# A Hymba layer on one core: weights of the first half fetched three ahead and split in turn, short convolution weight by weight, output splits in quarters

## The chip, the cores and the metric

The kernel runs on one core of a Trainium2 chip. The metric is the device time of one execution in microseconds (us), taken as the median of several runs. One launch computes everything; nothing is computed on the host.

## The reference

One layer of a backbone that mixes a short gated convolution with a bidirectional mLSTM, and then has a feed-forward part. There are 128 context tokens and 2048 latent tokens with 1024 features, in float32. Cut to its core:

```python
h = rmsnorm(x, norm1) * (1 + scale1) + shift1
z = h @ w_in                                    # sc_b, sc_c, sc_x, q, k, v, o, gates
y_sc = sc_b * conv3(sc_c * sc_x, conv_sc_w, conv_sc_b)
h_m = mlstm_bidir(q, k, v, gates, C0, n0, m0)   # 4 heads of 128, chunks of 128 tokens, both directions
h_m = rmsnorm_per_head(h_m) * mh_norm * sigmoid(o)
x = x + gate1 * (concat(y_sc, h_m) @ w_out)
h2 = rmsnorm(x, norm2) * (1 + scale2) + shift2
up = conv3(h2 @ w_up)
x = x + gate2 * ((silu(g) * a) @ w_down)        # a, g are the halves of up
```

The mLSTM goes through the chunks of 128 tokens with a matrix state: each chunk's output takes an attention-like product inside the chunk, weighted by exponentials of the gates, and a product with the state; each chunk's gated sum of k and v then updates the state. The results are both token groups after a final norm and the context's final states.

## The kernel before

**Tiling.** Features lie on the 128 partitions, tokens along the free dimension. The 2176 tokens are cut into blocks `BL` of 384 (the last has 256). Blocks 0, 1, 2 (`BA`) are called the first half, 3, 4, 5 (`BB`) the second. Every matrix product takes both operands as a high and a low part (fp32r) and makes three products of them. `load_w` fetches a weight tile of 1024 x 128 (512 KB) to `wst` (L103, two buffers), takes the high part on ScalarE (`wh`, L105) and the difference on GpSimd in two pieces of 512 columns (`wl`, L108). `gemm` (L191 to L199) makes 8 x 3 = 24 matmuls (L196, L197, L198) into one PSUM bank `acc`; "block product" below means such a group of 24.

**Order of the work.** Everything is written as generators that yield after each block product, so that other work can be put between. The second half goes first: v and gates, k heads, q heads, short convolution, o heads. Then the first half: v and gates (`vg`, evacuated by `rv`, L338); the gate rows (`gate_phase`), whose logarithm is taken by two activations (L589, L590, each with a table load) and which transposes `fc` and `ic` (L598), with k heads between its steps. Then come two passes by `weave`, a software pipeline over 34 units (17 chunks x 2 pairs of heads):

- `Sums`: transposes of k (`S`, L697), their copy `kT` on ScalarE, the weighted values `vw` on VectorE (L701), the product `y` (L708) and the update of the state `sb` (L721).
- `Mix`: `load` issues the loads of k, q, v, the state and `R` (L742, the gate rows of a chunk, 512 KB broadcast to all partitions). `first` makes `S` = q k (L753), adds the mask to `R` on GpSimd (L754), takes four exponentials on ScalarE (L758) and two products on VectorE (L761, L762). `second` makes the output products `y` (L773, L775), takes the denominators (L783 to L785), and empties `y` through ScalarE (L790) and VectorE (L791) into `hv`, then takes the norm (L793 to L797). `third` transposes `hv` (L803), multiplies it with the o gate (L805) and writes it to `yD` (L808).

In step i of `weave` unit i does `first`, i-3 `third`, i-1 `second` and i+1 `load`; then block products of the `fill` generator follow: 12 of q heads, 12 of o heads, 36 of the short convolution and 32 of the output projection of blocks 0 to 3. `Sums` takes one per step, `Mix` one per step and one more in every third. So in `Mix` the steps carry 2, 1, 1.

**Buffers.** PSUM has four banks `acc`, one tile `y` of two banks (a bank for each head), one bank `S` and one bank `st`. Split weights have four buffers.

**Output projection.** `out_proj` takes its blocks in pairs. For a pair it loads `yD` (`xt`, L404), splits all eight features of both blocks on ScalarE and VectorE (`hH` L406, `hL` L407), then for each of eight weights makes both blocks' products. It adds the residual (L433), writes `xD` (L435) and sums squares (L440, L441). The statistics of a pair (`inv_rms`, L122 to L126) follow; for the last pair (4, 5) they are put off into the FFN, to its fifth product (index 4).

**FFN.** The up projection runs by seven products of half size (L938 to L940); the token sums they need are written to `tD` and loaded as `slots` (L252, L257, L258). One product of a pair of blocks is 24 matmuls of 272 columns. The down projection is at L1030 to L1032.

Each engine runs its instructions in the order the scheduler wrote, and SP issues all transfers from one queue in order; an issue that waits for a buffer holds what is behind it.

Of the kernel before, what the change touches and what calls it, by code (L numbers as in the profile page):

```python
# [18 lines left out]
P = 128  # L19
# [11 lines left out]
WN = 1056  # L31
BL = [(i, min(384, T - i)) for i in range(0, T, 384)]
# [21 lines left out]
def hymba_kernel(ctx: ExitStack, tc: tile.TileContext, I, O):  # L54
# [46 lines left out]
    def load_w(src, n=1024):  # L101
        st = wp.tile([P, WN], F32, name="wst", bufs=2)
        Q.dma_start(st[:, :n], src)  # L103
        wh = wp.tile([P, WN], F32R, name="wh")
# [11 lines left out]
    def inv_rms(ss, n, r):  # L116
        """r [n tokens as columns of 128] = rsqrt(mean + eps) from the partial sums ss [P, n]."""
# [10 lines left out]
    def spread(r, n):  # L128
        """PSUM [P, n]: the columns of r along the free dimension, on every partition."""
# [60 lines left out]

    def gemm(w, h, n):  # L191
        (wh, wl), (hH, hL) = w, h
        acc = pa.tile([P, 512], F32, name="acc")
# [66 lines left out]
    def weights(j):  # L260
        """The split weights of the seven products."""
# [29 lines left out]
    def stages():  # L291
        """Products of all units, in order, each with its weights."""
        for hf in range(2):
            for j in range(FT):
                for i, w in enumerate(weights(j)):
                    yield hf, j, i, w

    # ---------------------------------------------------------------- mixer
    ph2 = ExitStack()
    with ExitStack() as ph1:  # L300
        wp = ph1.enter_context(tc.tile_pool(name="wp", bufs=4))
        xp = ph1.enter_context(tc.tile_pool(name="xp", bufs=2))
        pa = ph1.enter_context(tc.tile_pool(name="pa", bufs=4, space=PSUM))
# [5 lines left out]
        rq = ph0.enter_context(tc.tile_pool(name="rq", bufs=2))  # L309
# [13 lines left out]
        def vg(blocks, hs, ws):  # L323
            for b in blocks:
                hH, hL = hs[b]
                for j in range(2):
                    for c in chunks(b):
                        o = c * P - BL[b][0]
                        acc = pa.tile([P, 512], F32, name="acc")
# [21 lines left out]
        def heads(blocks, hs, w0, dst, func, scale, by_block=False):  # L351
            if by_block:
                ws = [load_w(I["w_in"][w0 + h]) for h in range(H)]
# [5 lines left out]
            for h in range(H):  # L359
                w = load_w(I["w_in"][w0 + h])  # L360
# [4 lines left out]
        def shortconv(blocks, hs):  # L365
            for m in range(4):
                wc, wx, wb = (load_w(I["w_in"][o + m]) for o in (4, 8, 0))
                for b in blocks:
                    t0, n = BL[b]
                    acc = gemm(wc, hs[b], n)  # L370
                    cr = rq.tile([P, 384], F32, name="cr")
                    S.activation(cr[:, :n], acc[:, :n], AF.Copy)
                    yield
                    acc = gemm(wx, hs[b], n)
                    V.tensor_tensor(cr[:, :n], acc[:, :n], cr[:, :n], op=ALU.mult)
                    yr = rq.tile([P, 384], F32, name="yr")
                    S.activation(yr[:, :n], cr[:, :n], AF.Identity, bias=scw[:, m, 3:4], scale=scw[:, m, 1:2])
                    for s0, s1, v in spans(t0, t0 + n):
                        w = GW if v else P
                        uu = cr[:, s0 - t0:s1 - t0].rearrange("p (r w) -> p r w", w=w)  # L380
                        yy = yr[:, s0 - t0:s1 - t0].rearrange("p (r w) -> p r w", w=w)
                        V.scalar_tensor_tensor(yy[:, :, 1:], uu[:, :, :w - 1], scw[:, m, 0:1],
                                               yy[:, :, 1:], op0=ALU.mult, op1=ALU.add)
                        V.scalar_tensor_tensor(yy[:, :, :w - 1], uu[:, :, 1:], scw[:, m, 2:3],
                                               yy[:, :, :w - 1], op0=ALU.mult, op1=ALU.add)
                    yield
                    acc = gemm(wb, hs[b], n)
# [751 lines left out]
```

## Time and profile before

| | us |
|---|---|
| median of 3 runs | 2620.94 (2619.29 to 2621.29) |
| profiled execution, span from first to last instruction | 2622.1 |
| TensorE busy | 2539.1 (97%) |
| VectorE busy | 1501.3 (57%) |
| ScalarE busy | 1066.1 (41%) |
| GpSimd busy | 706.4 (27%) |
| mean granted TensorE clock | 0.988 of full |

The profiled execution's own time is its span of 2622.1 us; the page gives no time around it. PE is TensorE, PEld its weight loads, DVE VectorE, ACT ScalarE, POOL GpSimd, SP the queue that issues transfers. In a row of waits stands who waited, for which engine and tile, the total, how often and the longest, in us. In a row of the timeline stand start, length, engine, line, operation, output and inputs, and in brackets the idle time before and what ended it. In a row of a window stand its bounds and length, then the busy time of each engine with its instructions, the granted clock, the share of the DMA engines and GB/s.

### The profile page before, as it was taken

The page shows a single profiled execution, that of the slowest core. Times are in us where ns is not written, and L with a number is a line of the kernel's source. Part 1 is how long each engine was busy: PE and PEld are TensorE (multiplying, and loading weights), DVE is VectorE, ACT ScalarE, POOL GpSimd, SP SyncE. Part 2 cuts the span into 40 slices and gives each one's busy share as a digit, 9 for nine tenths or more (in the row PEclk, how much of TensorE's full clock was granted, in tenths as well). Part 3 has the DMA queues.
Part 4 walks back from the last instruction along what each step waited for, and adds up shares of the span by engine and source line. Part 5 has one row for each costly group of instructions (what it writes and reads, how often), then busy time and mean ns, then how long its engine had stood idle before and what let it go on. Part 6 is the DMA issues. An engine that isn't in the chain of part 4 may idle for free. (4 is left out here: it accounts for less than half of the span.)

```text
span 2622.1 us, 46918 instructions
## 1 busy us (share of the span) xinstructions
PE 2539.1 (97%) x18511; PEld 2519.2 (96%) x18511; DVE 1501.3 (57%) x2560; ACT 1066.1 (41%) x2028; POOL 706.4 (27%) x534
## 2 busy tenths in 40 slices
PE   8999999999988988899999999999999999999998
PEld 7999999999988988899999999999999999999998
DVE  3993242333457666797686669666666635353533
ACT  4521142322345454464454446554544523232411
POOL 2542242211333344221121112111111222232232
PEclk9999999999999999999999999999999999999999
DMA  8773142555467887854252224222222635454442
GB/s 280 250 254 101 57 140 85 155 180 155 152 195 242 253 256 235 267 195 139 84 178 91 79 79 165 83 83 82 83 83 90 234 113 184 156 179 150 149 139 77
DMA packets 223582, 403.25 MB, mean 154 GB/s; under 512 B 20722, under 2 KB 144770, under 8 KB 221698
## 3 DMA queue, kind: packets, MB, share of 16 engines
q1 hardware_dynamic: 223362, 400.25, 46.5%
q8 instruction: 145, 2.38, 0.4%
q14 instruction: 75, 0.61, 0.1%
HBM read 305.13 MB, written 95.04 MB: 153 GB/s over the span
## 5 line engine op out<-in xcount | busy, mean ns | idle before, releaser
L196 PE MATMUL acc<-hH,wh 128*128 128x384 f32 (+1 forms) x1536 | 516.4, 336 | 0.0
L198 PE MATMUL acc<-hH,wl 128*128 128x384 f32 (+1 forms) x1536 | 505.0, 329 | 0.0
L197 PE MATMUL acc<-hL,wh 128*128 128x384 f32 (+1 forms) x1536 | 504.7, 329 | 0.0
L938 PE MATMUL pa<-tH,wh 128*128 128x272 f32 x1408 | 410.1, 291 | 5.6 <-DVE raw L950 5.2
L940 PE MATMUL pa<-tH,wl 128*128 128x272 f32 x1408 | 409.3, 291 | 0.4 <-DVE wl L276 0.4
L1030 PE MATMUL d<-uh,wh 128*128 128x272 f32 x1408 | 406.0, 288 | 3.1 <-ACT raw L948 3.1
L939 PE MATMUL pa<-tL,wh 128*128 128x272 f32 x1408 | 407.1, 289 | 0.0
L1032 PE MATMUL d<-uh,wl 128*128 128x272 f32 x1408 | 406.9, 289 | 0.0
L1031 PE MATMUL d<-ul,wh 128*128 128x272 f32 x1408 | 404.4, 287 | 0.0
L276 POOL TENSOR_TENSOR wl<-st,wh 128x512 fp32r<-128x512 f32 x132 | 182.3, 1381 | 730.5 <-ACT wh L275 697.5
L108 POOL TENSOR_TENSOR wl<-wst,wh 128x512 fp32r<-128x512 f32 (+1 forms) x160 | 234.3, 1486 | 434.0 <-ACT wh L105 421.5
L196 PEld LDWEIGHTS acc<-hH,wh 128*128 128x128 f32 x1536 | 291.1, 190 | 1.5 <-issue 0.4
L197 PEld LDWEIGHTS acc<-hL,wh 128*128 128x128 f32 x1536 | 291.1, 189 | 1.0
L198 PEld LDWEIGHTS acc<-hH,wl 128*128 128x128 f32 x1536 | 290.5, 189 | 0.2 <-issue 0.2
L938 PEld LDWEIGHTS pa<-tH,wh 128*128 128x128 f32 x1408 | 266.8, 190 | 6.4 <-issue 5.7
L1030 PEld LDWEIGHTS d<-uh,wh 128*128 128x128 f32 x1408 | 266.9, 190 | 3.4 <-ACT raw L948 3.3
L939 PEld LDWEIGHTS pa<-tL,wh 128*128 128x128 f32 x1408 | 267.3, 190 | 0.0
L940 PEld LDWEIGHTS pa<-tH,wl 128*128 128x128 f32 x1408 | 266.6, 189 | 0.6 <-DVE wl L276 0.6
L1032 PEld LDWEIGHTS d<-uh,wl 128*128 128x128 f32 x1408 | 266.1, 189 | 0.1
L1031 PEld LDWEIGHTS d<-ul,wh 128*128 128x128 f32 x1408 | 265.3, 188 | 0.0
L993 POOL TENSOR_TENSOR wl<-st,wh 128x704 fp32r<-128x704 f32 x64 | 150.5, 2352 | 367.2 <-ACT wh L991 358.2
L884 DVE SCALAR_TENSOR_TENSOR tt<-raw,fw,tt 128x127 f32<-128x127 f32 (+4 forms) x264 | 245.7, 959 | 1.5 <-ACT tt L890 0.8
(215 smaller groups left out, 5031.6 us busy)
## 6 DMA issues: line engine op xcount, KB each, us to landing
st<-in_w_up SPq DMA_DIRECT2D x88, 512.0 KB, 4.4
st<-in_w_down SPq DMA_DIRECT2D x64, 704.0 KB, 4.2
wst<-in_w_in SPq DMA_DIRECT2D x48, 512.0 KB, 4.1
us<-uD SPq DMA_DIRECT2D x88, 272.0 KB, 4.4
R<-nD SPq DMA_DIRECT2D x34, 512.0 KB, 5.5
wm<-in_w_modr SPq DMA_DIRECT2D x32, 512.0 KB, 4.7
F<-tD SPq DMA_DIRECT2D x12, 1088.0 KB, 8.8
uD<-tt SPq DMA_DIRECT2D x22, 576.0 KB, 2.8
```

The source lines that it names most:

```text
L108: G.tensor_sub(wl[:, a:a + n // 2], st[:, a:a + n // 2], wh[:, a:a + n // 2].bitcast(F32))
L196: PE.matmul(acc[:, :n], w_h, hH[:, k, :n], start=(k == 0), stop=False)
L197: PE.matmul(acc[:, :n], w_h, hL[:, k, :n], start=False, stop=False)
L198: PE.matmul(acc[:, :n], w_l, hH[:, k, :n], start=False, stop=(k == KT - 1))
L276: (G if on_pool else V).tensor_sub(wl, a, wh.bitcast(F32))
L884: V.scalar_tensor_tensor(o, i, w, o, op0=ALU.mult, op1=ALU.add)
L938: PE.matmul(acc, wh[:, w], rh, start=(kk == 0 and i in (0, 1, 5)), stop=False, skip_group_check=True)
L939: PE.matmul(acc, wh[:, w], rl, start=False, stop=False, skip_group_check=True)
L940: PE.matmul(acc, wl[:, w], rh, start=False, stop=(kk == 3), skip_group_check=True)
L1030: PE.matmul(acc[b][:, :NB], wh[:, c], uh[:, q], start=(j == 0), stop=False)
L1031: PE.matmul(acc[b][:, :NB], wh[:, c], ul[:, q], start=False, stop=False)
L1032: PE.matmul(acc[b][:, :NB], wl[:, c], uh[:, q], start=False, stop=(j == FT - 1))
```

## The change

Nine things change; the products computed stay the same.

1. **Weights of the first half.** A class `Stream` fetches the weights in the order of their use, as long as fewer than three are fetched or split, and splits the next one when one is taken. `in_turn` ties a split to the last ScalarE and the last GpSimd instruction written so far: it stays behind these in its engine's order. Split weights have five buffers instead of four.
2. **Short convolution** goes through the blocks with one weight, then with the next, instead of through three weights in each block (`cr`, `yr`: four buffers).
3. **Output projection.** The order is weights 0 and 1 on the first block, then on the second, then weight by weight. `split_y` splits a block in quarters (two features each). The quarters of the second block come beside the first two products, the rest of them at once before its first; those of the next pair's first block beside the last four products of this one. Rows of x are loaded two products ahead.
4. **PSUM.** Three pools of one bank for `acc`, taken in turn (a fourth bank during the start); `y` is one bank per head in a ring of three.
5. **`Sums` and `Mix`** work per head on `y`, and in `Mix` the state update `sf` stands behind the evacuation.
6. **`weave`** takes 1, 0, 1 fills in `Sums` (by step modulo three, from step -1) and 2, 1, 2 in `Mix`.
7. **Late statistics** of the last pair come after the FFN's second product (index 1), with their instructions placed behind its last matmul.
8. The FFN's loads and weight sums move with these, as the scheduler orders them.
9. The scratch for dynamic DMA is set to 1024; texts in the code are dropped.

```diff
-    def load_w(src, n=1024):
+    def in_turn(f, *engines):
+        traced = nc.cur_bb.bb.instructions
+        n, last = len(traced), {}
...
+        r = f()
+        for i in traced[n:]:
+            if i.engine in last:
+                tc.add_manual_dep(i, last[i.engine], mybir.DependencyInfo(
+                    mybir.DependencyClass.NoSync, mybir.DependencyReason.DATA), reason="in turn")
...
+    class Stream:
+        def fill(self):
+            while len(self.st) + len(self.ws) < 3:
+                src = next(self.srcs, None)
...
+                self.st.append(fetch(src))
+        def split(self):
+            if self.st:
+                st = self.st.pop(0)
+                self.ws.append(in_turn(lambda: split_w(st), ET.Activation, ET.Pool))
+        def __call__(self):
+            self.fill()
+            if not self.ws:
+                self.split()
+            w = self.ws.pop(0)
+            self.split()
+            self.fill()
+            return w
...
-        wp = ph1.enter_context(tc.tile_pool(name="wp", bufs=4))
+        wp = ph1.enter_context(tc.tile_pool(name="wp", bufs=5))
-        pa = ph1.enter_context(tc.tile_pool(name="pa", bufs=4, space=PSUM))
+        pa = [ph1.enter_context(tc.tile_pool(name=f"pa{i}", bufs=1, space=PSUM)) for i in range(3)]
...
+        def split_y(b):
+            yH, yL = ys[b] = h_pair()
+            for kh in range(2):
+                yt = xp.tile([P, 4, 384], F32, name="xt")
+                Q.dma_start(yt[:, :, :n], yD[4 * kh:4 * kh + 4, :, t0:t0 + n].rearrange("k p t -> p k t"))
+                for k in range(4):
+                    S.activation(yH[:, 4 * kh + k, :n], yt[:, k, :n], AF.Copy)
+                    V.tensor_sub(yL[:, 4 * kh + k, :n], yt[:, k, :n], yH[:, 4 * kh + k, :n].bitcast(F32))
+                    if k % 2:
+                        yield
...
+                order = [(0, b0), (1, b0), (0, b1), (1, b1)] + [(m, b) for m in range(2, KT) for b in (b0, b1)]
...
+                    if i < 2:
+                        run(islice(splits[b1], 2))
+                    elif after is not None and i >= 12:
+                        splits.setdefault(after, split_y(after))
+                        next(splits[after], None)
...
+        py = phr.enter_context(tc.tile_pool(name="py", bufs=3, space=PSUM))
...
-                pk = pm.tile([P, 2, 512], F32, name="y")
+                pk = [py.tile([P, 512], F32, name="y") for _ in range(2)]
...
-                y = pm.tile([P, 2, 512], F32, name="y")
+                ys = [py.tile([P, 512], F32, name="y") for _ in range(2)]
...
-                next(fill, None)
-                if extra and i % extra == 0:
+                for _ in range(blocks[i % 3]):
                     next(fill, None)
...
-        weave([Sums(c, hp) for c in range(NL - 1, -2, -1) for hp in range(2)], fill, 0)
-        weave([Mix(c, hp) for c in range(-1, NL) for hp in range(2)], fill, 3)
+        weave([Sums(c, hp) for c in range(NL - 1, -2, -1) for hp in range(2)], fill, (1, 0, 1))
+        weave([Mix(c, hp) for c in range(-1, NL) for hp in range(2)], fill, (2, 1, 2))
...
-            if late and i == 4:
-                late.pop()()
...
+            if late and i == 1:
+                with tc.issue_after(mm.ins):
+                    late.pop()()
```

At the start of the gates ScalarE had the splits `wh` of the first weights between the evacuations `rv` of the values, ahead of the two gate activations (`fe`, table load and activation twice). Before:

```order
L338 ACTIVATE rv<-acc 128x2x128 x12
L105 ACTIVATE wh<-wst 128x1024
L338 ACTIVATE rv<-acc 128x2x128
L105 ACTIVATE wh<-wst 128x1024
L338 ACTIVATE rv<-acc 128x2x128 x2
L105 ACTIVATE wh<-wst 128x1024
L338 ACTIVATE rv<-acc 128x2x128
L105 ACTIVATE wh<-wst 128x1024
L589 ACT_TABLE_LOAD
L589 ACTIVATE fe<-fe 128x136
L590 ACT_TABLE_LOAD
L590 ACTIVATE fe<-fe 128x136
```

Now, on the same engine at the same place (the lines are L393, L155, L672 and L673):

```order
L393 ACTIVATE rv<-acc 128x2x128 x16
L672 ACT_TABLE_LOAD
L672 ACTIVATE fe<-fe 128x136
L673 ACT_TABLE_LOAD
L673 ACTIVATE fe<-fe 128x136
L155 ACTIVATE wh<-wst 128x1024 x2
L403 ACTIVATE row<-acc 128x384 x3
```

The splits of the first weights went behind both gate activations. On TensorE, the transpose of `fc` stood behind two block products of the k head (the rows are the end of the second); `ic` followed three matmuls later:

```order
L198 MATMUL acc<-hH,wl 128x384
L598 MATMUL S<-ident,fc 128x128
L196 MATMUL acc<-hH,wh 128x384
L197 MATMUL acc<-hL,wh 128x384
L198 MATMUL acc<-hH,wl 128x384
L598 MATMUL S<-ident,ic 128x128
```

Now it stands straight behind the last product of the values (L388 to L390), and the k head's products (L250 to L252) begin behind it; `ic` follows after two of them:

```order
L388 MATMUL acc<-wh,hH 128x264
L389 MATMUL acc<-wl,hH 128x264
L390 MATMUL acc<-wh,hL 128x264
L681 MATMUL S<-ident,fc 128x128
L250 MATMUL acc<-hH,wh 128x384
L251 MATMUL acc<-hL,wh 128x384
```

Two block products went from ahead of the transpose of `fc` to behind it. In `Sums`, on TensorE, a block product used to follow each unit's products; before:

```order
L198 MATMUL acc<-hH,wl 128x384
L697 MATMUL S<-ident,k_5138 128x128 x2
L708 MATMUL y<-vw,kT 128x258 x2
L196 MATMUL acc<-hH,wh 128x384
L197 MATMUL acc<-hL,wh 128x384
```

Now, at a step without a fill (S is the transpose of a unit's k, y the product of the unit before):

```order
L780 MATMUL S<-ident,k_5039 128x128 x2
L791 MATMUL y<-vw,kT 128x258 x2
L780 MATMUL S<-ident,k_5095 128x128 x2
L791 MATMUL y<-vw,kT 128x258 x2
L250 MATMUL acc<-hH,wh 128x384
```

Two units' products stand together, with no block product between them. At the FFN's start, on TensorE, the first late statistics (`st` from `ss`) stood between the last output product and the first FFN product:

```order
L198 MATMUL acc<-hH,wl 128x256
L122 MATMUL st<-ones,ss 128x1 x3
L938 MATMUL pa<-tH,wh 128x272
L939 MATMUL pa<-tL,wh 128x272
L940 MATMUL pa<-tH,wl 128x272
```

Now the FFN begins straight behind the output product, and the statistics come 48 matmuls later, behind its second product (`pb`):

```order
L1025 MATMUL pb<-tL,wh 128x272
L1026 MATMUL pb<-tH,wl 128x272
L172 MATMUL st<-ones,ss 128x1 x3
L1024 MATMUL pa<-tH,wh 128x272
L1025 MATMUL pa<-tL,wh 128x272
L1026 MATMUL pa<-tH,wl 128x272
```

The statistics went from ahead of two FFN products to behind them.

More of the change, by code (lines that the diff above doesn't have):

```diff
@@ L189, in make_h, with accumulator @@
         return apply(b, load_x(b, src, xp, "xt", 2), norm)
+    def accumulator():
+        pool = pa[next(turn_a) % len(pa)]
+        return pool.tile([P, 512], F32, name="acc")
     def gemm(w, h, n):
         (wh, wl), (hH, hL) = w, h
-        acc = pa.tile([P, 512], F32, name="acc")
+        acc = accumulator()
         for k in range(KT):
@@ L328, in vg @@
                         o = c * P - BL[b][0]
-                        acc = pa.tile([P, 512], F32, name="acc")
+                        acc = accumulator()
                         for k in range(KT):
@@ L445, in out_proj @@
                 else:
-                    stats(grp, sss)
+                    last()
         hs = {}
-        with tc.tile_pool(name="start", bufs=1, side="right") as stp:
+        with tc.tile_pool(name="start", bufs=1, side="right") as stp, \
+                tc.tile_pool(name="pj", bufs=1, space=PSUM) as pj:
+            pa.append(pj)
             def mod_pe(mt):
@@ L453, in mod_pe @@
                 Q.dma_start(st, I["w_mod"][mt])
-                ps = pa.tile([P, 512], F32, name="acc")
+                ps = accumulator()
                 for k in range(KT):
@@ L808, in third, with weave @@
                 Q.dma_start(yD[4 + 2 * hp:6 + 2 * hp, :, t0:t0 + P].rearrange("h d t -> d h t"), o2)
-        def weave(units, fill, extra):
+        def weave(units, fill, blocks):
             n = len(units)
@@ L862, in hymba_kernel @@
         late = []
-        last = out_proj(((4, 5),), late)
+        last = out_proj(((4, 5),), take, defer=late)
         run(islice(last, 1))
```

221 lines of the change are left out of this document (125 added, 96 removed).

## Prediction

> **What bounds the kernel now.** I read the page first.
>
> ```profile
> PE 2539.1 (97%) x18511; PEld 2519.2 (96%) x18511; DVE 1501.3 (57%) x2560; ACT 1066.1 (41%) x2028; POOL 706.4 (27%) x534
> ```
>
> TensorE is busy for 2539.1 of 2622.1 us, and the change keeps its products. What can be won is the 83 us in which it is idle, and the time in which it is busy at a lower clock. Who it waits for says where the idle time lies:
>
> ```profile
> PE y L773 <- DVE hv L791: 33.3, 14, 6.9
> PE st L122 <- DVE ss L441: 8.3, 3, 6.5
> PE acc L334 <- POOL wl L108: 1.0, 1, 1.0
> ```
>
> The 33.3 us are 14 waits of the output products of `Mix` for the one PSUM tile `y`. Of the rest 6.5 us are one wait of the late statistics. Then the busy time by stretches: `Sums` with k and q heads (440 to 660), `Mix` (700 to 1000), and single stretches of 10 us behind long waits. Columns are the stretch and its length, the busy time of PE, PEld, DVE, ACT and POOL with counts, the granted clock, the DMA share and GB/s.
>
> ```profile
> 440.00:660.00 220.00, 218.67 (x1237) 211.12 (x1236) 73.03 (x163) 63.86 (x147) 43.87 (x31) 0.99 0.51 156
> 700.00:1000.00 300.00, 266.30 (x1705) 262.80 (x1705) 189.31 (x489) 152.89 (x467) 116.30 (x102) 0.96 0.75 235
> 760.00:770.00 10.00, 6.45 (x36) 6.25 (x35) 3.83 (x13) 3.53 (x11) 4.01 (x4) 0.83 0.65 185
> 820.00:830.00 10.00, 6.96 (x37) 7.00 (x38) 9.92 (x20) 6.76 (x19) 5.46 (x5) 0.83 0.53 174
> 850.00:860.00 10.00, 7.99 (x44) 7.78 (x43) 5.32 (x18) 4.83 (x17) 2.41 (x3) 0.83 0.78 234
> 870.00:880.00 10.00, 7.99 (x44) 7.78 (x43) 7.36 (x20) 5.02 (x15) 5.35 (x5) 0.83 0.67 200
> 930.00:940.00 10.00, 7.18 (x31) 7.21 (x32) 6.00 (x19) 5.57 (x18) 4.33 (x4) 0.56 0.68 198
> 950.00:1000.00 50.00, 44.44 (x301) 43.63 (x300) 32.09 (x81) 25.24 (x75) 23.47 (x21) 1.00 0.84 264
> 1110.00:1120.00 10.00, 7.26 (x33) 7.29 (x34) 5.92 (x10) 3.67 (x6) 0.85 (x1) 0.51 0.87 313
> ```
>
> `Sums` is full: 1.3 us idle in 220. One product there takes 218.67/1237 = 0.177 us, so a block product of 24 takes 4.2 us. `Mix` is idle for 33.7 us in 300 and loses clock besides. The timeline gives the waits that stand ahead of those slow stretches, and one that has none behind it:
>
> ```profile
> 764.41 0.47 PE L773 MATMUL y<-sf,qs 128*128 128x129 f32 x2 [3.55 <-DVE hv L791]
> 823.03 0.77 PE L773 MATMUL y<-sf,qs 128*128 128x129 f32 x2 [4.74 <-DVE hv L791]
> 852.40 0.46 PE L773 MATMUL y<-sf,qs 128*128 128x129 f32 x2 [2.01 <-DVE hv L791]
> 873.68 0.52 PE L773 MATMUL y<-sf,qs 128*128 128x129 f32 x2 [2.01 <-DVE hv L791]
> 932.82 0.77 PE L773 MATMUL y<-sf,qs 128*128 128x129 f32 x2 [6.89 <-DVE hv L791]
> 998.28 0.46 PE L773 MATMUL y<-sf,qs 128*128 128x129 f32 x2 [3.06 <-DVE hv L791]
> ```
>
> Why DVE is late shows in the stretch before 764.41, followed through the queues:
>
> ```profile
> 750.33 2.54 POOL L108 TENSOR_TENSOR wl<-wst,wh 128x512 fp32r<-128x512 f32 x2 [2.26 <-ACT wh L105]
> 752.90 0.35 SPq L103 DMA_DIRECT2D wst<-in_w_out  x1
> 753.81 0.42 SPq L742 DMA_DIRECT2D R<-nD  x1
> 759.52 1.72 POOL L754 TENSOR_TENSOR R<-R,maskN 128x512 f32<-128x512 f32 x1 [5.71 <-DMA R<-nD]
> 761.27 1.28 ACT L758 ACTIVATE R<-R,cols 128x128 f32<-128x128 f32 x4 [5.19 <-POOL R L754]
> 762.46 0.34 ACT L790 ACTIVATE hv<-y,den 128x128 f32<-128x128 f32 x1
> 763.91 0.35 DVE L791 SCALAR_TENSOR_TENSOR hv<-y,den,hv 128x128 f32<-128x128 f32 x1 [0.72 <-ACT hv L790]
> SPq L103 <- POOL wl L108: 23.0, 9, 4.6
> ```
>
> The weight fetch stands on SP's queue until POOL has split an older weight (752.90), so the load of `R` behind it is issued late. It lands 5.7 us on. POOL adds the mask, ACT takes the exponentials, and only behind them on ACT stand the copies that empty `y` of the unit before. The next unit cannot start its products until the last of them, at 764.26. So the wait is a chain with a length of about one unit's time, and the units with one block product each are too short for it. (The last row of the fence is SP's own sum of such waits.)
>
> **Part by part.** The sum is made against the span of 2622.1 us; the median of the runs is 2620.94, 1.2 below, and I take the difference off that.
>
> *Fills and banks in `Mix`.* Steps carried 2, 1, 1 block products in turn and now 2, 1, 2; the shortest pair of steps goes from two products to three, 4.2 us more. Besides, `y` is a bank per head in a ring of three, so the first head of the next unit need not wait for both heads. A wait shrinks by up to 4.2 us: of the 14 only 4.74 and 6.89 are longer, and leave 0.5 and 2.7. I take -31. Bounds: if only the mean gain of a third of a product (1.4 us) counts, 14 x 1.4 = 19.6, so -20; all gone is -33.
>
> *Clock behind the waits.* Each of the four stretches at 0.83 has lost 0.17 x 10 = 1.7 us. That at 0.56 was at half clock for 8.8 us, of which 2.8 are wait, so 3.0 us of busy time are lost: 9.8 together. With the waits nine tenths of it go: -9, bounds -5 (two windows stay) and -9.8.
> The rows at 852.40 and 873.68 show that a wait of 2.01 us is already followed by a slow stretch, while 3.06 at 998.28 has none (1.00 over 950 to 1000). [...]
>
> *Output splits in quarters.* The splits of a group's y come in quarters among the group before, only the first group's first block at once. The rows that hold this work:
>
> ```profile
> L407 DVE TENSOR_TENSOR hL<-xt,hH 128x384 fp32r<-128x384 f32 x40 | 24.6, 632 | 8.2 <-ACT hH L406 8.0
> xt<-yD SPq DMA_DIRECT2D x10, 768.0 KB, 5.6
> ```
>
> One block is 8 such splits, 5.1 us of DVE, behind two loads of 5.6 us. The waits of 4.74 and 6.89 lie at the two group starts in `Mix`, so part of them was this work. Quarters (1.3 us) fit beside a product of 4.2; the eager block and the second block, finished just ahead of its first use, can still make TensorE wait: +4, from 0 (hidden, as most of it is now) to +10 (one load and one split bare).
>
> *`Sums`.* Fills go from one per step to 1, 0, 1, so in 12 steps S and K products of two units follow each other with nothing between.
>
> ```profile
> 538.23 0.38 PE L697 MATMUL S<-ident,k 128*128 128x128 f32 x2
> 538.45 1.04 PE L708 MATMUL y<-vw,kT 128*128 128x258 f32 x4
> 539.52 0.69 DVE L701 TENSOR_TENSOR vw<-v,cols 128x516 f32<-128x516 f32 x1 [3.04 <-PE y L708]
> 540.13 0.60 DVE L721 SCALAR_TENSOR_TENSOR sb<-sb,decB,y 128x129 f32<-128x129 f32 x2
> 534.20 1.76 DVE L701 TENSOR_TENSOR vw<-v,cols 128x516 f32<-128x516 f32 x1 [4.04 <-PE y L708]
> ```
>
> The next unit's `vw` starts when K ends (539.49) and takes 0.69; the S products fill 0.22 of that. K's second head then also needs a third and fourth bank of three, freed by a DVE step of 0.30 behind `vw`. So 0.5 for the first and 0.3 for the second, 0.8 x 12 = +10. Bounds: +6 (0.5 each); +20 if `vw` takes 1.76 each time, as beside a split of a weight.
>
> *Start of the gates.* The order now has the transpose of `fc` straight behind the last vg product, and the weight splits of the first k head behind the two gate activations on ACT, where two block products and a split stood between.
>
> ```profile
> 428.85 0.39 ACT L338 ACTIVATE rv<-acc 128x256 f32<-128x256 f32 x1 [0.53 <-PE acc L335]
> 429.13 1.05 ACT L105 ACTIVATE wh<-wst 128x1024 fp32r<-128x1024 f32 x1
> 431.01 1.32 DVE L588 SCALAR_TENSOR_TENSOR fe<-fc 128x136 f32<-128x136 f32 x1
> 433.99 0.32 ACT L590 ACTIVATE fe<-fe 128x136 f32<-128x136 f32 x1
> 436.84 0.27 PE L598 MATMUL S<-ident,fc 128*128 128x128 f32 x1
> ```
>
> TensorE would be idle from 428.85. The logarithm ends at 434.31, the split on ACT at 435.4, the first POOL half (2.54/2 = 1.27) at 436.6, where the third product needs it: 6.5 idle plus 0.9, so 7.4. If DVE and the table loads go 2 us faster without a split beside them, 5.5. A gap so long brings a slow stretch, 1.7 to 3.0. I take +8, bounds +5 and +11. Nothing covers this; the products that did are still there behind it.
>
> *Late statistics.* They move from ahead of the FFN's first product to behind its second.
>
> ```profile
> 1112.74 1.41 PE L122 MATMUL st<-ones,ss 128*128 128x1 f32 x6 [6.54 <-DVE ss L441]
> ```
>
> Two FFN products (48 matmuls) now run in that wait: 6.54 gone, and with it the half clock that the 0.51 in 1110 to 1120 shows, 4.9 us of deficit less 2.7 of wait, halved by the products that follow: 2.4. Next late are the token sums of the third product, which TensorE reaches earlier by the same time. I take -7, bounds -9 and -3.
>
> *Nothing or little.* A fifth buffer for split weights lets a vg weight be split earlier: the wait for `wl` of 1.0 above, -1, bounds -1 and +1. Short convolution by weight has the same products, hidden under them. The third block's accumulator, three banks instead of four, is covered by an evacuation of 0.5 us against 4.2. Streamed fetches stand as many on SP as before.
>
> Sum: -31 - 9 + 4 + 10 + 8 - 7 - 1 = **-26**, so 2620.94 - 26 = **2595 us**.
>
> **Rivals.**
> *New waits in `Mix` (B).* With three banks and splits tied to the last instruction traced, a third of the 40 us (waits and clock) comes back as other waits: -26 + 13, **2608**. For it: DVE is busy 189 of 300 us and the waits of 4.74 and 6.89 have splits in them. Against: the longer pair of steps covers 12 of 14.
> *The ring stays closed (C), slower.* The split on POOL now stands in turn behind the mask addition, which waits for `R`; the next fetch waits for the split, the next `R` behind the fetch. One turn is 5.7 + 1.7 + 2.5 = 9.9 us, against 6.8 for a step of one product and 11 for two. Where each fetch falls on a short step, the 40 us stay and the costs remain: -26 + 40 = +14, **2635**. It decides from 26 us of waits in `Mix` on. For it: the 23.0 us on SP's queue. Against: two of three steps are now longer than the turn, and fetches run three ahead.
> *No change (D).* The loads of `R` are bound by the DMA, so 22 us of waits stay, their clock loss of 5 too: -11 - 4 + 14 = -1, **2620**. Against: 235 GB/s in `Mix`, 264 in the stretch from 950, so the engines can move more; and the same bytes now have more time.
>
> **How the numbers follow.** Forecast 0.66, B 0.15, D 0.10, C 0.09. All bounds to the good give about 2580, and 2618 takes in B and the poor ends one or two at a time, so 2580 to 2618 leaves out D, C and the tail. A difference under 0.2% (5.2 us) cannot be told from no change. Faster by more: forecast and B with few exceptions, 0.80; within: D and the edge of B, 0.11; slower: C, 0.09.
>
> **What the new profile would show.** Right: waits of `y` below 6 us in all; granted clock 0.99 or more from 700 to 1000; a gap of 5 to 8 us ahead of the first k head; twelve gaps of about 0.8 us in `Sums`, for K; no wait of 6.5 for the late statistics. Wrong: SP's queue held by the weight splits longer than 23 us and `y` still waiting (C); new names, `acc` or `hL` of the y splits, with over 10 us in TensorE's waits (B); or `R` landing over 6 us after its issue (D).

## The result and the profile after

The changed kernel takes 2654.83 us (median of four runs, 2646.73 to 2655.83), the kernel before 2621.11 in the same series. The ratio is 1.0119 with a 95% interval of 1.0105 to 1.0133: slower by 1.2%, where 2595 us was forecast. The profiled execution is the fastest of the four (2646.73 us, span 2644.9); its sums therefore explain 22.8 us of the 33.7 between the medians. One execution of a later kernel (e14) took 4376.88 us at a mean granted clock of 0.706; no ratio counts it, though the median of e14 does.

The page of the changed kernel. Busy time of TensorE rose by 10.1 us with the same products, and its idle time from 83.0 to 95.7:

```profile
span 2644.9 us, 46918 instructions
PE 2549.2 (96%) x18511; PEld 2525.1 (95%) x18511; DVE 1486.9 (56%) x2662; ACT 1072.0 (41%) x2062; POOL 694.4 (26%) x534
```

TensorE's waits in the changed kernel. Before, `y` stood first with 33.3 us. It is at 1.6 now, and other names stand in its place:

```profile
PE acc L250 <- ACT wh L155: 10.1, 4, 6.3
PE st L271 <- ACT rb L273: 9.9, 1, 9.9
PE acc L250 <- ACT hH L469: 6.3, 1, 6.3
...
PE st L172 <- DVE ss L511: 4.9, 1, 4.9
PE st L890 <- DVE den L867: 4.9, 2, 2.6
PE acc L252 <- POOL wl L158: 4.5, 8, 0.7
PE S L681 <- DVE fc L674: 4.2, 1, 4.2
PE st L172 <- DVE o L892: 4.2, 1, 4.2
...
PE S L780 <- ACT kT L782: 3.5, 1, 3.5
...
PE y L861 <- DVE hv L871: 1.6, 1, 1.6
```

Three instructions of TensorE stand at places where the same number of block products is done in both kernels (61 and 145 of 384 columns with 24 of 256, then 160 and 32): the first transpose of `Sums`, the last state product of `Mix`, the first FFN product. In the timeline of the kernel before they are

```profile
490.71 0.38 PE L697 MATMUL S<-ident,k 128*128 128x128 f32 x2
1009.65 0.39 PE L773 MATMUL y<-sf,qs 128*128 128x129 f32 x2
1114.02 0.57 PE L938 MATMUL pa<-tH,wh 128*128 128x272 f32 x1
```

and in the changed kernel

```profile
495.03 0.38 PE L780 MATMUL S<-ident,k 128*128 128x128 f32 x2
1014.49 0.39 PE L861 MATMUL y<-sf,qs 128*128 128x129 f32 x2
1140.13 0.39 PE L1024 MATMUL pa<-tH,wh 128*128 128x272 f32 x1 [0.58 <-DVE row L503]
```

So 4.3 us are lost up to `Sums`, 0.5 in the two passes together, 21.3 between the last `y` and the FFN, and 3.3 are won from there to the end: 22.8. These three bounds give the stages of the kernels below, except for one shift in e12 that is named there ("gates" is the time of the first row, "passes" from the first to the second, "late" from the second to the third, "FFN" the rest of the span).

The late stage shows how the time is lost. TensorE is idle there for 24.1 us, against 9.3 before and 8.4 in the kernel without the tie (e1 below), and the same products take 101.5 us of busy time instead of 95.0 and 94.7, at a mean clock of 0.88 instead of 0.96 and 0.97. Against e1, the waits for `wh` and `wl` are 8.6 us instead of none, the one for `rb` 9.9 instead of 4.9, and the one for `ss` 4.9 instead of 1.2. The timeline of the changed kernel shows the wait for `rb` (first row, taken up at e6), and then what stands ahead of the longest wait for `wh`, through all engines:

```profile
1073.48 1.54 PE L271 MATMUL st<-ident,rc 128*128 128x80 f32 x6 [9.93 <-ACT rb L273]
...
1079.99 0.33 SPq L120 DMA_DIRECT2D wst<-in_w_out  x1
...
1101.16 0.85 SPq L278 DMA_DIRECT2D F<-xD  x2
1102.98 0.78 DVE L283 SCALAR_TENSOR_TENSOR F<-F,ab,rb 128x544 f32<-128x544 f32 x1 [2.49 <-DMA F<-xD]
1103.80 0.75 ACT L285 ACTIVATE F<-F,modT 128x544 f32<-128x544 f32 x1 [3.90 <-DVE F L283]
1104.89 0.75 ACT L285 ACTIVATE F<-F,modT 128x544 f32<-128x544 f32 x1
1105.67 0.91 ACT L293 ACTIVATE tH<-F 128x272 fp32r<-128x272 f32 x2
1106.48 1.04 ACT L155 ACTIVATE wh<-wst 128x1024 fp32r<-128x1024 f32 x1
1107.58 0.69 PE L250 MATMUL acc<-hH,wh 128*128 128x384 f32 x1 [6.34 <-ACT wh L155]
```

The split `wh` of the output weight stands on ScalarE behind the token sums (L285, L293). These wait for VectorE (L283), and that for a load. The weight's fetch had been issued at 1079.99, and such fetches land 4.3 us after their issue by the median of this profile (6.3 us in the one landing it times between 1070 and 1110); ScalarE was idle for 3.90 us ahead of the token sums while the weight lay ready. The tie keeps the split behind the ScalarE instruction that was written last before it, and what was written last here was the side work (the token sums) that `out_proj` of blocks 4 and 5 is woven with.

### The profile page after: what moved, and what is told of

Its sections match the earlier page's. It is cut to its first block, busy times and chain, and to the rows that moved or that the text cites. A ratio compares the mean times of both kernels' runs of the same rounds, so it can differ in the third digit from the quotient of the medians.

```text
span 2644.9 us, 46918 instructions
## 1 busy us (share of the span) xinstructions
PE 2549.2 (96%) x18511; PEld 2525.1 (95%) x18511; DVE 1486.9 (56%) x2662; ACT 1072.0 (41%) x2062; POOL 694.4 (26%) x534
## 5 line engine op out<-in xcount | busy, mean ns | idle before, releaser
L250 PE MATMUL acc<-hH,wh 128*128 128x384 f32 (+1 forms) x1536 | 521.0, 339 | 16.5 <-ACT wh L155 10.1
L252 PE MATMUL acc<-hH,wl 128*128 128x384 f32 (+1 forms) x1536 | 510.7, 333 | 4.5 <-POOL wl L158 4.5
L158 POOL TENSOR_TENSOR wl<-wst,wh 128x512 fp32r<-128x512 f32 (+1 forms) x160 | 224.9, 1428 | 381.0 <-ACT wh L155 306.2
L250 PEld LDWEIGHTS acc<-hH,wh 128*128 128x128 f32 x1536 | 294.7, 192 | 19.1 <-ACT wh L155 11.4
L252 PEld LDWEIGHTS acc<-hH,wl 128*128 128x128 f32 x1536 | 293.3, 191 | 7.7 <-POOL wl L158 7.5
```

The source lines that it names most:

```text
L158: G.tensor_sub(wl[:, a:a + n // 2], st[:, a:a + n // 2], wh[:, a:a + n // 2].bitcast(F32))
L250: PE.matmul(acc[:, :n], w_h, hH[:, k, :n], start=(k == 0), stop=False)
L252: PE.matmul(acc[:, :n], w_l, hH[:, k, :n], start=False, stop=(k == KT - 1))
```

## The experiments

Sixteen kernels ran in four series (e1 to e4, e5 to e8, e9 to e12, e13 to e16), each with the kernel before on one chip. Medians are compared inside a series, and across series by the ratio to the kernel before. Stages are in us from each one's profiled execution, which can lie some us off the median (e4 most: 2676.21 against 2667.35):

| kernel | median | ratio (95%) | gates | passes | late | FFN |
|---|---|---|---|---|---|---|
| before | 2621.11 | 1 | 490.7 | 518.9 | 104.4 | 1508.1 |
| changed | 2654.83 | 1.0119 (1.0105 to 1.0133) | 495.0 | 519.5 | 125.6 | 1504.8 |
| e1 no tie | 2604.35 | 0.9925 (0.9904 to 0.9947) | 488.1 | 503.0 | 103.1 | 1507.6 |
| e2 tie in the passes | 2623.23 | 1.0004 (0.9993 to 1.0014) | 486.1 | 518.4 | 106.6 | 1509.9 |
| e3 tie at gates, passes | 2638.42 | 1.0056 (1.0037 to 1.0075) | 494.6 | 519.9 | 109.6 | 1509.0 |
| e4 tie, old fills | 2667.35 | 1.0174 (1.0150 to 1.0198) | 496.0 | 546.3 | 122.1 | 1509.9 |
| e5 tie on ScalarE | 2654.96 | 1.0128 (1.0103 to 1.0152) | 493.6 | 531.2 | 122.0 | 1505.4 |
| e6 tie on GpSimd | 2651.11 | 1.0115 (1.0094 to 1.0137) | 492.1 | 515.5 | 133.5 | 1506.3 |
| e7 no tie, old fills | 2610.49 | 0.9952 (0.9939 to 0.9966) | 488.1 | 507.0 | 102.8 | 1508.2 |
| e8 no tie, late fifth | 2608.85 | 0.9952 (0.9936 to 0.9968) | 488.7 | 505.9 | 104.1 | 1508.1 |
| e9 no tie, early gate | 2613.74 | 0.9968 (0.9957 to 0.9979) | 489.5 | 511.3 | 104.5 | 1508.5 |
| e10 no tie, no Stream | 2610.86 | 0.9965 (0.9952 to 0.9978) | 489.5 | 511.1 | 101.7 | 1511.0 |
| e11 no tie, two banks | 2608.41 | 0.9958 (0.9943 to 0.9972) | 488.8 | 505.5 | 104.3 | 1508.5 |
| e12 before, tie added | 2682.39 | 1.0247 (1.0223 to 1.0271) | 486.7 | 571.7 | 115.8 | 1506.3 |
| e13 = e1 again | 2609.89 | 0.9957 (0.9942 to 0.9972) | 490.4 | 506.4 | 104.0 | 1510.9 |
| e14 no tie, no Stream, old fills | 2608.31 | 0.9952 (0.9939 to 0.9965) | 485.3 | 508.6 | 104.9 | 1506.2 |
| e15 = e8 again | 2610.10 | 0.9961 (0.9949 to 0.9972) | 489.8 | 506.1 | 102.9 | 1509.5 |
| e16 = e9 again | 2613.17 | 0.9973 (0.9961 to 0.9986) | 489.4 | 507.7 | 105.4 | 1512.0 |

In e12 four block products of the gates come behind the first bound instead of ahead of it (57 and 88 products of 384 columns, where all others have 61 and 84). At the 4.2 us that the prediction works out for one, an estimated 17 us of its passes belong to its gates.

The theory (T) after the result: the tie makes the kernel slower. Its rivals: A, three accumulator banks and the new order of the output projection; Q, fetches three ahead on SP's queue.

**e1: the tie undone.**

```diff
-                self.ws.append(in_turn(lambda: split_w(st), ET.Activation, ET.Pool))
+                self.ws.append(split_w(st))
```

> The changed kernel with one thing undone: the weight splits of the first half are no longer tied behind the last ScalarE and GpSimd instruction written. Theory T (the tie puts the splits on ScalarE behind work that itself waits for transfers): TensorE's waits for wh, wl and rb between the last output product of the mixer and the first FFN product (about 20 us and their slow stretches) go, the wait of 4.2 us for fc goes, and so do the short waits for wl in the output projection: 2608 to 2622 us. Rival A (three accumulator banks and the new order of the output projection make the late stage slow): it stays within 4 us of the changed kernel, 2650 to 2656. Rival Q (transfers: weights three ahead hold SP's queue): also 2650 or more, with the waits moved to DMA.

Measured 2604.35 us, ratio 0.9925. With one line undone the kernel is faster than before by 0.75%, and by the ratios some 50 us faster than with the line. Its three bounds:

```profile
488.14 0.38 PE L780 MATMUL S<-ident,k 128*128 128x128 f32 x2
991.11 0.39 PE L861 MATMUL y<-sf,qs 128*128 128x129 f32 x2
1094.21 0.39 PE L1024 MATMUL pa<-tH,wh 128*128 128x272 f32 x1 [2.40 <-DVE row L503]
```

All three stages are shorter than in the changed kernel: gates by 6.9 us, passes by 16.5, late by 22.5. In TensorE's waits of this kernel `wh` and `wl` of the mixer and `fc` no longer appear with half a microsecond; these are left:

```profile
PE st L271 <- ACT rb L273: 4.9, 1, 4.9
...
PE acc L250 <- ACT hH L469: 4.6, 1, 4.6
PE y L861 <- DVE hv L871: 4.0, 5, 1.2
...
PE st L172 <- DVE o L892: 3.4, 1, 3.4
...
PE y L791 <- DVE sb L805: 2.0, 3, 0.7
```

A and Q both expected 2650 or more; their parts are all still in this kernel. T holds.

**e2 and e3: the tie by place.** A flag `pin` chooses between the two lines of e1; it is set only during the two passes (e2), or from the gates to the end of the passes (e3).

```diff
-                self.ws.append(in_turn(lambda: split_w(st), ET.Activation, ET.Pool))
+                self.ws.append(in_turn(lambda: split_w(st), ET.Activation, ET.Pool) if self.pin else split_w(st))
...
+        take.pin = True
         weave([Sums(c, hp) for c in range(NL - 1, -2, -1) for hp in range(2)], fill, (1, 0, 1))
         weave([Mix(c, hp) for c in range(-1, NL) for hp in range(2)], fill, (2, 1, 2))
+        take.pin = False
```

> The tie is kept only while the two passes Sums and Mix are woven with block products; the k heads at the start of the gates and what follows the passes are free of it. Theory T: the late stage comes back to about 97 us (from 125) and the wait for fc goes, the waits inside Mix stay: 2618 to 2630 us. Rival A or Q: 2648 to 2656.

> The tie is kept at the start of the gates and in the passes, and dropped behind them. Theory T: only the late stage comes back, 25 to 28 us, so 2624 to 2632 us, and it is 4 to 8 us (wait for fc and its slow stretch) above the kernel with the tie in the passes alone. Rival A or Q: 2650 to 2656.

e2 is at 2623.23 us, as theory T expected, and e3 at 2638.42, 6 us above its range; it was expected 4 to 8 us above e2 and is 15.2 above it. Against e1 on the same chip the tie in the passes costs 18.9 us, at the gates 15.2 more, and behind the passes, by the ratios (1.0119 less 1.0056), 16.5 more. The stages agree for two of the three: passes 503.0 to 518.4 from e1 to e2, late 109.6 to 125.6 from e3 to the changed kernel. The gates grow from 486.1 to 494.6 from e2 to e3, 8.5 us; the rest of that step lies behind them. In none of the three places does the tie gain.

**e4: old fills, tie kept.**

```diff
-        weave([Sums(c, hp) for c in range(NL - 1, -2, -1) for hp in range(2)], fill, (1, 0, 1))
-        weave([Mix(c, hp) for c in range(-1, NL) for hp in range(2)], fill, (2, 1, 2))
+        weave([Sums(c, hp) for c in range(NL - 1, -2, -1) for hp in range(2)], fill, (1, 1, 1))
+        weave([Mix(c, hp) for c in range(-1, NL) for hp in range(2)], fill, (2, 1, 1))
```

> The changed kernel with the old fills: one block product per step in Sums, and 2, 1, 1 in Mix. If the fills are what took away the waits for y (my prediction), these come back, 10 to 25 us, and the kernel is at 2660 to 2675 us. If the ring of three banks and the order on VectorE took them away, the waits for y stay under 5 us and the time stays at 2646 to 2658.

2667.35 us; by the ratios (1.0174 to 1.0119) some 14 us more than the changed kernel. The waits for `y` are back at 19.0 us in ten. With the tie the new fills are worth that much.

**e5 and e6: which queue.** The tie on one engine only.

```diff
-                self.ws.append(in_turn(lambda: split_w(st), ET.Activation, ET.Pool))
+                self.ws.append(in_turn(lambda: split_w(st), ET.Activation))     # e5
+                self.ws.append(in_turn(lambda: split_w(st), ET.Pool))           # e6
```

> The changed kernel with the splits tied to the last ScalarE instruction alone, not to GpSimd's. If the harm is done on ScalarE's queue (the high part stands behind the token sums, the exponentials and the gate activations, which wait for others): as slow as the changed kernel, 2640 to 2656 us. If it is done on GpSimd's queue (the low part behind the mask addition, which waits for R, as in rival C of the prediction): 2604 to 2615 us.

> The tie to the last GpSimd instruction alone. The counterpart: 2602 to 2612 us if ScalarE's queue does the harm, since GpSimd is 73% idle and its splits already follow ScalarE's; 2635 to 2656 if GpSimd's does.

2654.96 and 2651.11 us: each half of the tie alone costs as much as both. I had set one queue against the other, and both do the harm. With the tie on GpSimd alone the wait is for the low part, and the one for `rb` is there as well:

```profile
PE acc L252 <- POOL wl L158: 15.6, 6, 5.4
PE st L271 <- ACT rb L273: 10.6, 2, 9.5
```

A block product takes both parts of its weight, so it waits for the part that is tied; the other part, done early, does not help. `rb` is not tied at all, and its wait stands in e1 too, at 4.9 us. It is longer here because of the order that the scheduler made: with tied splits it puts the transposes of `rc` (L271) on TensorE ahead of block products, and TensorE, in order, stands at the second of them until the one bank `st` is emptied by `rb`. In the order without the tie 3.8 block products stand between the last two of these groups ahead of the FFN (two of them of 256 tokens), in the changed kernel one short one. So the tie costs time in two ways, by the split that is late and by the order that follows from it; the two were not separated by a run.

**e7: old fills without the tie.** The edits of e1 and e4 together.

> The kernel without the tie, with the old fills (1 per step in Sums; 2, 1, 1 in Mix). By the first terms of my sum the fills are worth 20 to 30 us net (waits for y and slow stretches come back, 2 to 10 us of gaps in Sums go): 2620 to 2635 us, with waits for y over 15 us. If the banks per head and the order on VectorE do it, 2600 to 2610 and waits for y under 8 us.

2610.49 us, ratio 0.9952, against 0.9925 for e1 in another series and 0.9957 for the same kernel as e1 in a third (e13). Waits for `y` in this kernel:

```profile
PE y L861 <- DVE hv L871: 10.0, 8, 2.7
```

With the old fills 23 of the 33 us are gone already. The fills are worth a few microseconds at most here (passes 507.0 against 503.0 and 506.4), not 20 to 30.

**e8 and e15: late statistics at the fifth product again, without the tie.**

```diff
+            if late and i == 4:
+                late.pop()()
...
-            if late and i == 1:
-                with tc.issue_after(mm.ins):
-                    late.pop()()
```

> The kernel without the tie, with the late statistics again at the FFN's fifth product. By my term of 7 us (bounds 3 and 9): 2607 to 2613 us, with a wait of 4 to 7 us for ss ahead of the FFN's first product. If that wait only moves to the third product's token sums, 2602 to 2606.

> Without the tie, late statistics at the fifth product, on the same chip as the one with them at the second. By my term of 7 us: 5 to 9 us above it. By the two profiles, in which the stretch from the last y to the FFN differed by 1 us: within 3 us of it.

2608.85 us in one series; in another, beside the kernel of e1, 2610.10 against 2609.89. Moving the statistics is worth nothing that can be told here. The wait of 6.5 us for `ss` ahead of the FFN does not return with the old place: something else in the change took it away. The new order of the output projection is a likely cause, but it was not tried alone.

**e9 and e16: block 0's last short-convolution product two block products earlier, without the tie.** In the fourth row of the convolution the third weight is taken behind the second weight's first block, and block 0 is finished there.

```diff
+                    if m == 3 and b == 0:
+                        wb = take()
+                        gate(b)
+                        yield
...
```

> The kernel without the tie, and with one product moved: the last product of the short convolution on block 0 comes two block products earlier, so that block 0's rows are written about 8 us sooner and the first split of the output projection finds them. If the wait of 4.6 us for hH at its start (with 1.1 for hL and a slow stretch behind it) is the age of these rows: 2595 to 2601 us, and the wait gone. If the split has to wait for its turn on ScalarE or for the loads: 2602 to 2606.

> Without the tie, block 0's last short-convolution product two earlier, on the same chip. If the wait that it takes away is truly given back (waits of 4.8 for den and 5.8 for o of the statistics came in its place): 3 to 9 us above the kernel without the tie. If that was chance: within 3 us of it or faster.

2613.74 us, slower than either of my ranges for e9, and 2613.17 us in the second series, beside 2609.89. The wait for `hH` that it aims at falls (7.2 to 0.6 in the series where both ran), and others take its place. In the profile of e16:

```profile
PE st L172 <- DVE o L903: 5.8, 1, 5.8
...
PE st L901 <- DVE den L878: 4.5, 1, 4.5
```

The edit moved a wait, and gained nothing.

**e10, e11 and e14: the other parts undone, without the tie.** e10 drops `Stream` (a weight is fetched and split when taken), e11 gives `y` two banks instead of three, e14 is e10 with the old fills.

```diff
-            take = Stream(srcs + [I["w_out"][m] for _ in range(3) for m in range(KT)])
+            plain = (load_w(s) for s in srcs + [I["w_out"][m] for _ in range(3) for m in range(KT)])
+            take = lambda: next(plain)
```

```diff
-        py = phr.enter_context(tc.tile_pool(name="py", bufs=3, space=PSUM))
+        py = phr.enter_context(tc.tile_pool(name="py", bufs=2, space=PSUM))
```

> The kernel without the tie and without the class Stream: each weight is fetched and split when it is taken, as in the second half. If fetching three ahead was worth something, the waits for y and wl in Mix grow and the time is 2608 to 2618 us. If the scheduler moves the splits ahead by itself and the five buffers allow it: 2600 to 2607.

> The kernel without the tie, with a ring of two banks for y instead of three. The old fills alone left 10 us of waits for y where the kernel before had 33, so the banks (or the order on VectorE) must have taken most. If the third bank does it: waits for y and for K in Sums of 12 to 25 us in all, 2612 to 2625 us. If one bank per head is enough: 2603 to 2609.

> Without the tie, without Stream, and with the old fills: what is left is the banks, the order of short convolution and output projection, the quarters and the late statistics. If these carry the gain: waits for y 8 to 14 us, 0.995 to 0.998. If Stream and the fills carry it: waits for y over 20 us, 0.999 to 1.003.

2610.86, 2608.41 and 2608.31 us. All ratios lie between 0.9952 and 0.9965, and their intervals overlap with that of e13. My ranges for e7 to e11 were set from the 2604.35 us of e1; beside the ratio of e13, the 2610.86 of e10 shows no worth of `Stream`, though it lies in the range that I had set for one. The fetches three ahead, the third bank and the new fills each make no difference that can be told once the tie is gone. In e14, with fetches and fills undone, 8.3 us of waits for `y` remain. So the gain over the kernel before (0.3 to 0.75%) most likely belongs to what all these kernels share: `y` evacuated head by head from banks of its own, `sf` behind that, the order of the short convolution and of the output projection, the splits in quarters, the buffers of `acc` and of the split weights. Which of these it is was not tried.

**e13: the kernel of e1 again.**

> The kernel without the tie, once more, beside the three below on the same chip. If its 2604 us is its own and not that chip's: a ratio to the kernel before of 0.990 to 0.995. If kernels without the tie differ among themselves only by chip and placement: 0.995 to 0.997, as the three runs of the last call.

2609.89 us, ratio 0.9957, on another chip. The first ratio of 0.9925 was partly that series': the same program's waits for `y` are 8.5 us here and 4.0 there, for `hH` 7.2 and 4.6. Taken from e13 by the ratios, the tie costs 42 us in the whole instead of 51, and 12 in the passes instead of 19.

**e12: the kernel before with the tie and nothing else.** `in_turn` goes into `load_w`, from the k heads of the first half on.

```diff
     def load_w(src, n=1024):
         st = wp.tile([P, WN], F32, name="wst", bufs=2)
         Q.dma_start(st[:, :n], src)
+        return in_turn(lambda: split_w(st, n), mybir.EngineType.Activation, mybir.EngineType.Pool) if tie else split_w(st, n)
...
         run(vg(BA, hs, load_vg(0) + load_vg(1)))
+        tie.append(1)
```

> The kernel before with one thing added: the splits of the first half's weights, from the k heads at the gates on, are tied to the last ScalarE and GpSimd instruction written. Theory T: the tie harms by itself, 2640 to 2675 us, with waits for wh or wl in the output projection and a wait for fc. If it harms only with the new order of the work: 2616 to 2630.

2682.39 us, ratio 1.0247, above my range: the tie alone costs the old kernel 62 us, more than it costs the new one, which at least splits one use ahead. The waits of this kernel:

```profile
PE acc L217 <- ACT wh L126: 19.3, 16, 2.7
PE y L794 <- DVE hv L812: 18.7, 12, 3.8
PE acc L219 <- POOL wl L129: 13.3, 20, 3.3
PE st L238 <- ACT rb L240: 8.3, 1, 8.3
```

Here the splits stand behind what was written just before their use, and the product follows at once: 36 waits for `wh` and `wl`. The old and the new order of the work both suffer, so it is the tie and not its company.

## Why the prediction was wrong, point by point

The step that failed is the last of the sum, "nothing or little", which left the tie at nothing outside the gates. The terms for the passes were over-valued besides.

- **Fills and banks, -31.** The waits for `y` did fall from 33.3 to 1.6 us. But the passes took 519.5 us instead of 518.9: with the tie the time came back under other names (`hH` 6.3, `den` 4.9, `o` 4.2, `kT` 3.5, and of `wh` and `wl` 5.5). Of these `hH` and `o` stand without the tie as well (4.6 and 3.4 in e1, 7.2 and 2.4 in e13). Without it the passes take 503.0 to 506.4, 12 to 16 us less than before, about a third to two fifths of the 40 that I had for waits and clock: this term was over-valued, tie or not. The working was wrong as well: e7 and e14 show 23 to 25 us of the 33 gone with the old fills, so the longer pair of steps was not what removed most of them. (The two remainders of 0.5 and 2.7 would also have left 30.1, not 31.)
- **Clock, -9.** In the changed kernel slow stretches stand behind new waits (a clock of 0.83 over the 10 us behind 3.51 us of wait up to 503.13, 0.84 behind 6.28 us up to 841.47), as they stood behind the old. The mean clock fell from 0.988 to 0.982; without the tie it is 0.988 to 0.994. From 700 to 1000 it is 0.95 where it was 0.96 and 0.99 was expected, and 0.97 without the tie.
- **Splits in quarters, +4.** The wait for the eager block is 6.3 us, with 1.2 for `hL`: inside the bounds of this term.
- **`Sums`, +10.** Wrong: the twelve gaps of 0.8 us are not there. No unit waits there in the changed kernel but one, for 3.5 us, for `kT` that stands on ScalarE behind exponentials of `Mix`; without the tie three waits of 0.7 for `sb`, 2.0 in all. I took the start of `vw` behind K for a need of the next K, but `vw` is made a unit ahead: in the pair at 517.88 the second K uses the one of 512.70.
- **Start of the gates, +8.** Right in mechanism: a gap of 4.20 us ahead of `fc`, a little under the 5 to 8 that I had, and the stretch from 430 to 440 at 0.66 of the clock. The size is 4.3 us from the kernel before to the changed one, 6.9 against e1 and 8.5 from e2 to e3.
- **Late statistics, -7.** The wait went, but not through the move (e15). The 2.4 in it for the clock was no clean sum: by the way of the clock term (9.8 us at half clock, which the windows of 2 us from 1110 to 1118 show as 0.50; 2.7 of them wait) it would be 3.5.
- **"Nothing or little" is the step that failed.** "Streamed fetches stand as many on SP as before" looked at the fetches, and not at the split that is tied; outside the gates the tie stood in the sum at nothing. I had followed it to the gates, where the listing showed it, and not to the two places where it does the same: the block products inside `Mix`, and the stage ahead of the FFN, where the last instruction written is a token sum that waits for a load. The runs put 12 to 19 us on the first of these and 16.5 on the second, where the late stage went from 104.4 to 125.6 us.
- **Rival B** named the tie too, and new waits in `Mix`, and that is where 12 to 19 us came back, near its 13. But it stopped at `Mix` and left the rest of the sum as it was, so its 2608 us had the wrong sign too.
- **Rival C** had the right sign and named the tie, at 2635 us, but put the price on `R` and `y`. SP did stand longer for the splits, by its own waits from 650 to 1130 us, in the kernel before, in the changed one and in e1:

```profile
SPq L103 <- POOL wl L108: 24.8, 12, 4.6
SPq L103 <- ACT wh L105: 6.0, 3, 3.8
```

```profile
SPq L120 <- POOL wl L158: 66.3, 28, 4.0
SPq L120 <- ACT wh L155: 32.2, 14, 6.4
```

```profile
SPq L120 <- POOL wl L158: 32.1, 13, 4.3
SPq L120 <- ACT wh L155: 27.5, 8, 6.6
```

  It did not keep `y` waiting: 1.6 us with 98.5 us of this on SP. The harm came through TensorE's own need for the tied weights and through the order around them. That C had the sign right is luck as far as its path goes.
- **Rival D** expected `R` over 6 us after its issue; its median in the changed kernel is 5.8.

With the tie taken out of the sum (8 for the gates) the forecast would have been -34; the kernel without it gains 9 to 18. What remains is the part by which I over-valued the passes and the late statistics, less most of the 10 for `Sums`, which were not there.

## What to carry to other kernels

A dependency that only fixes an order is not free (here it cost 42 to 51 us): it can put an instruction that is ready behind one that is not, with the engine idle between (here ScalarE for 3.90 us). When a change ties something to "the last instruction written", list at every place of the program what that instruction is and what it waits for, side work of other stages included, and price the slowest. A wait that goes from a list is no gain until the stage around it, between two instructions with the same work done, has become shorter.

## What the runs showed of the hardware

In the changed kernel a slow stretch stands behind waits of TensorE of 2.26 and 2.64 us, and none behind one of 1.73 us. These waits, and the windows that follow them:

```profile
809.52 0.41 PE L890 MATMUL st<-ident,hv 128*128 128x128 f32 x2 [2.26 <-DVE den L867]
881.67 0.41 PE L890 MATMUL st<-ident,hv 128*128 128x128 f32 x2 [2.64 <-DVE den L867]
909.99 0.44 PE L250 MATMUL acc<-hH,wh 128*128 128x384 f32 x1 [1.73 <-ACT wh L155]
```

```profile
810.00:820.00 10.00, 10.00 (x55) 9.90 (x54) 4.95 (x18) 3.99 (x14) 2.00 (x2) 0.83 0.79 256
880.00:890.00 10.00, 8.33 (x45) 8.36 (x46) 6.33 (x26) 4.29 (x15) 1.99 (x2) 0.83 0.84 261
910.00:920.00 10.00, 9.27 (x59) 8.95 (x60) 9.38 (x28) 5.69 (x18) 3.54 (x3) 1.00 0.77 249
1070.00:1080.00 10.00, 6.19 (x20) 5.68 (x21) 5.60 (x10) 4.54 (x8) 6.23 (x6) 0.50 0.73 232
```

2.26 and 2.64 us are followed by a clock of 0.83 over 10 us, 1.73 us by one of 1.00, and the wait of 9.93 us up to 1073.48 lies in a stretch at 0.50. The length of the wait does not decide alone: in the kernel before, 2.47 us up to 988.32 and 3.06 up to 998.28 have 1.00 over the 10 us behind them, where the shorter 2.26 us here have 0.83.

The medians of the same program without the tie differed by 5.5 us between two chips (2604.35 and 2609.89), while those of the kernel before stayed within 4 us between all series. The six executions of e13 on its one chip spread over more than that (2602.80 to 2613.50), so the difference need not be the chip's.
